# Another order, and a strict one, for the seven products of a Strassen-like matrix product

## The chip, the cores and the metric

The kernel runs on one core of one Trainium2 chip. The time is the device time of that core in microseconds (us). The engines are TensorE (PE, matmuls), VectorE (DVE), ScalarE (ACT), GpSimd (POOL) and SyncE (SP), whose queue issues most of the transfers. Each engine works through its own queue in a fixed order.

## The reference

A decoder trunk of two layers on 512 tokens with a model width of 1024. Each layer is a half-step feed-forward block, a mixing block with three kinds of attention, and a second half-step feed-forward block:

```python
def _swiglu(t, w_gate, w_up, w_down):
    return (jax.nn.silu(t @ w_gate) * (t @ w_up)) @ w_down

for l in range(DEPTH):
    f = _swiglu(_rmsnorm(h, ffn1_pre_g[l]), ffn1_w_gate[l], ffn1_w_up[l], ffn1_w_down[l])
    h = h + 0.5 * _rmsnorm(f, ffn1_post_g[l])
    ...   # mixing
    f = _swiglu(_rmsnorm(h, ffn2_pre_g[l]), ffn2_w_gate[l], ffn2_w_up[l], ffn2_w_down[l])
    h = h + 0.5 * _rmsnorm(f, ffn2_post_g[l])
```

`D_FF` is 2816, that is 22 blocks of 128 columns. All of it is in float32.

## The kernel before

**Precision.** A float32 factor is split into a high part (a cast on ScalarE, L182) and a low part (a subtraction on VectorE, L183). A product of two such factors is three matmuls, `mm3` (L203): high times high (L205), high times low weights (L206), low times high weights (L207).

**Seven products.** The first sixteen column blocks of a feed-forward block are computed as two chunks (`ci` 0 and 1) of 1024 columns. For each chunk, the gate and the up matrix product are done by a scheme with seven block products instead of eight, 0 to 6. This makes four groups of seven products in each feed-forward block, and there are four feed-forward blocks, named a0, c0, a1 and c1 in the tile names (so `pwc0g` is a bank of a gate group of block c0, `wh_gc` the high part of its weights). The block product with the down weights uses the same scheme (`product`, L851, tiles `pd`).

**Banks.** A product adds into a pair of PSUM banks. There are three pairs in a group: products 0, 3, 5 and 6 add into the first, 1 into the second, 2 and 4 into the third (`SUM`). After product 0 its two banks are copied to the second pair (L747). After each later product its pair is read out: copied by ScalarE after 2 and 3 (L775), added by VectorE after 4 and 5 (L777), and passed through the nonlinearity or multiplied after 1 and 6. A product that adds into a pair has to wait until the earlier read of that pair is done.

**Inputs.** Products 0, 1 and 6 take token blocks as they are (tiles `us`). Products 2, 3, 4 and 5 take sums of them (tiles `uh`, `ul`), which `sums` (L693) makes once per feed-forward block, step by step during the first group.

**Weights.** Each product has two units of weights (`BlockUnit`, L274), each 256 rows by 512 columns. A unit is fetched by a transfer on SP (L297), for products 2, 3, 5 and 6 combined with a kept block `t` by a subtraction on VectorE (L327), and split into `wh` and `wl`. Products 2 and 4 take over the raw block of 0 and 3. Raw blocks lie in two rings, `raw` with two buffers and `o` with four for this use; the kept blocks also have the tag `o`. The `wh` and `wl` tiles have four buffers each, that is two products. When a product begins, the next four units are loaded (`load_ahead`, L391), and when a raw buffer is released, the next unit in the order of the work is fetched if its ring has room (`fetch_ahead`, L411).

**Turned results.** The up groups hold their results with tokens on partitions; after products 1, 4, 5 and 6 they are transposed by transfers (`turn`, L790: copies L800, transposes L801 on SP, copies back L804 two products later). Products 1 and 5 use a tile with the tag `rs`, which has one buffer.

**The order of the work.** `PLAN` (L1643) lists the gate group of chunk 0, the up group of chunk 0, the gate group of chunk 1, the up group of chunk 1, then the down products with the remaining plain gate and up products between them. The program writes the instructions in this order, but the framework's scheduler may move an instruction ahead of others on its engine when it finds it ready sooner; a call of `keep_in_program_order` pins an instruction behind what was written before it on its engine.

Of the kernel before, what the change touches and what calls it, by code (L numbers as in the profile page):

```python
# [18 lines left out]
P = 128  # L19
# [4 lines left out]
def kernel(  # L24
# [85 lines left out]
    def pbank(tag, name):  # L110
        return ps.tile([P, S], F32, tag=tag, bufs=4, name=name)
# [88 lines left out]
        nc.vector.scalar_tensor_tensor(t, z, minus, t, ALU.max, ALU.add)  # L200
        nc.scalar.activation(t, t, AF.Exp, scale=-1.0, bias=minus)

    def mm3(pt, lh, ll, rh, rl, start, stop, free=False):  # L203

        nc.tensor.matmul(pt, lh, rh, start=start, stop=False, skip_group_check=free)  # L205
        nc.tensor.matmul(pt, lh, rl, start=False, stop=False, skip_group_check=free)  # L206
        nc.tensor.matmul(pt, ll, rh, start=False, stop=stop, skip_group_check=free)  # L207

# [386 lines left out]


    NG = 2
    ORDER = (0, 2, 1, 3, 4, 5, 6)
    SUM = (0, 1, 2, 0, 2, 0, 0)
    TO = ((0, 0), (0, 0), (1, 1), (0, 1), (0, 1), (1, 1), (1, 0))  # L600
    park = [nc.dram_tensor(f"park{i}", (NT, P, D), F32, kind="Internal").ap() for i in range(2 * L)]
# [1 line left out]
    def ffn(l, src, wg, wu, wd, dst, name, spare, parked, plan, aside=None):  # L603
# [136 lines left out]
        def token_product(ci, up, n, uns):  # L740

            nm = f"{name}{'gu'[up]}_{ci}_{n}"
            if n in (0, 1, 2):
                st["c", n] = [pbank("z" if n == 0 else "mm", f"pw{nm}_{e}") for e in range(2)]
            if n == 1:
                for e in range(2):
                    nc.scalar.copy(st["c", 1][e][:], st["c", 0][e][:])  # L747
            if n == 0:
                if not up:
                    st["s", ci] = {}  # L750
            pts = st["c", SUM[n]]
            h, l = in_product(n)
            opens, ends = n in (0, 2), n in (1, 4, 6)
            for un in uns:
                for k in range(un.nk):
                    kk = un.k0 + k
                    for e in range(2):
                        c = slice(e * P, (e + 1) * P)
                        mm3(pts[e][:], h[:, kk, c], l[:, kk, c], un.h[:, k], un.l[:, k], opens and kk == 0,
                            ends and kk == ND // 2 - 1, free=True)  # L760
                        yield 3 * S * PE_US
                    turn(kk)
            if n == 0:
                return
            q = TO[n]
            g = st["s", ci]
            if not up and q not in g:
                g[q] = stile([P, FC // 2, S // 2], "f", f"s{name}_{ci}_{q[0]}{q[1]}", F32)[:]
            g = g[q]
            r = hidden_rows(2 * ci + q[1])[:, :, HALVES[q[0]]] if up else g  # L770
            for e in range(2):
                p = pts[e][:].rearrange("p (f q) -> p f q", f=2)
                re, ge = r[:, 2 * e:2 * e + 2], g[:, 2 * e:2 * e + 2]
                if n in (2, 3):
                    nc.scalar.copy(re, p)  # L775
                elif n in (4, 5):
                    nc.vector.tensor_tensor(re, re, p, ALU.add)  # L777
                elif up:
                    nc.vector.tensor_tensor(ge, p, ge, ALU.mult)
                else:  # L780
                    nc.scalar.activation(re, p, AF.Silu)
            if n in (4, 5):
                if up:
                    nc.vector.tensor_tensor(g, r, g, ALU.mult)
                else:
                    nc.scalar.activation(r, r, AF.Silu)
            if up and n in (1, 4, 5, 6):
                turns.append([nm, g, (2 * ci + q[1], q[0]), n in (1, 5), 0, None])
# [21 lines left out]
        def token_products(ci, up):  # L810

            w, nm = (wu if up else wg)[l, :, ci * FC * P:(ci + 1) * FC * P], f"{'gu'[up]}{name}_{ci}"
            keep = Keep(lambda k0: stile([P, 2, S], "o", f"t{nm}_{k0}", F32)[:])
            places, had = itertools.cycle(("raw", "o", "o")), {}
            for n in ORDER:
                uns = [BlockUnit(n, w, ND // 2, k, 2, S, keep, f"{nm}_{n}_{k}", n in (2, 4) or next(places))
                       for k in range(0, ND // 2, 2)]
                if n in (2, 4):
                    for un, of in zip(uns, had[n - 2 + (n == 4)]):
                        un.inherits(of)  # L820
                had[n] = uns
                run = lambda n=n, uns=uns: token_product(ci, up, n, uns)
                early = ci == 0 and not up and n in ORDER[:4]
                yield uns, (lambda run=run: beside(run(), itertools.islice(st["some"], 1), 2)) if early else run

        def down_from(t, hf, pt):
# [24 lines left out]
        def product(at, uns):  # L851
# [10 lines left out]
            h, l = st.pop(("a", ci, n))  # L862
            opens, ends = first and n in (0, 2), last and n in (1, 4, 6)
            for un in uns:
                for k in range(un.nk):
                    kk = un.k0 + k
                    for e in range(2):
                        c = slice(e * P, (e + 1) * P)
                        mm3(pts[e][:], h[:, kk, c], l[:, kk, c], un.h[:, k], un.l[:, k], opens and kk == 0,
                            ends and kk == FC // 2 - 1, free=True)  # L870
                        yield 3 * S * PE_US
                    turn(kk)
            if not last:
                return
            if n == 0:
# [828 lines left out]
```

## Time and profile before

| | us |
|---|---|
| median of 3 runs | 2380.13 |
| the runs | 2378.37 to 2385.53 |
| the profiled execution | 2382.98 |
| its span, first to last instruction | 2380.9 |
| TensorE busy in the span | 2350.6 |
| VectorE busy | 1803.5 |
| ScalarE busy | 1513.8 |

The page gives the busy time of each engine; the list of waits says how long an engine stood idle before an instruction and what ended that; the timeline shows single instructions in order of time; windows give busy times of each engine in a stretch. Matmuls overlap in the trace: one row lasts 0.39 us, but the next begins before it ends, so the distance of the starts is what a matmul takes.

### The profile page before, as it was taken

The numbers are of one execution on the slowest core, as the hardware profiler recorded it, in microseconds if no ns is written. First come the engines' busy times: TensorE is split into PE (matmuls) and PEld (weight loads), VectorE is DVE, ScalarE is ACT, GpSimd is POOL, SyncE is SP. The second block draws the span as 40 slices with busy tenths as digits, with TensorE's granted clock in tenths as the row PEclk, the third lists the DMA queues.
The fourth block names the chain that finished last, engine by engine and source line by source line (L and its number), as shares of the span: only waits on it lengthen the run. The fifth ranks groups of instructions, "written<-read, shape, count | busy, mean of one in ns | idle before, by whom it ended". The sixth has DMA issues, their size and how long they took to land.

```text
span 2380.9 us, 31151 instructions
## 1 busy us (share of the span) xinstructions
PE 2350.6 (99%) x11719; PEld 1984.2 (83%) x11719; DVE 1803.5 (76%) x2358; ACT 1513.8 (64%) x2306; POOL 75.8 (3%) x134
## 2 busy tenths in 40 slices
PE   9999999999999999999999999999999999999998
PEld 7787889888888888778888878889888888888787
DVE  8886877667777689778788778766767767888785
ACT  6777465577766556775656665655777665567744
POOL 0000000000111000000000000000001100000000
PEclk9999999999999999999999999999999999999999
DMA  5666455223223556664647664542323235566643
GB/s 197 195 174 174 161 196 151 71 80 94 87 78 103 189 179 182 170 195 135 236 128 200 186 185 153 192 124 71 94 76 98 73 123 193 161 204 174 197 143 141
DMA packets 299754, 354.98 MB, mean 149 GB/s; under 512 B 78266, under 2 KB 192978, under 8 KB 299604
## 3 DMA queue, kind: packets, MB, share of 16 engines
q1 hardware_dynamic: 299508, 352.97, 48.0%
q8 instruction: 92, 1.51, 0.3%
q14 instruction: 58, 0.48, 0.1%
q0 software_dynamic: 96, 0.03, 0.0%
HBM read 319.39 MB, written 16.78 MB: 141 GB/s over the span
## 4 chain that ended last, share of the span: by engine, by line
PE 85%; DVE 5%; DMA 4%; ACT 4%; issue 2%; SPq 0%; DVEq 0%; ACTq 0%
PE pg L206 4%; PE pg L205 4%; PE pg L207 4%; PE pdc L206 3%; PE pdc L207 3%; PE pdc L205 3%; PE pda L206 2%; PE pda L207 2%; PE pda L205 2%; PE pb L207 2%; PE pb L206 2%; PE pb L205 2%; PE pq L206 1%; PE pq L205 1%; PE pk L207 1%
## 5 line engine op out<-in xcount | busy, mean ns | idle before, releaser
L205 PE MATMUL pg<-us_a,wh_wg 128*128 128x512 f32 x384 | 151.0, 393 | 0.0
L207 PE MATMUL pg<-us_a,wl_wg 128*128 128x512 f32 x384 | 149.8, 390 | 0.0
L206 PE MATMUL pg<-us_a,wh_wg 128*128 128x512 f32 x384 | 149.8, 390 | 0.0
L206 PE MATMUL pdc<-wl_dc,ahc 128*128 128x512 f32 x224 | 87.9, 392 | 3.6 <-DVE wl_dc L183 3.6
L206 PE MATMUL pda<-wl_da,aha 128*128 128x512 f32 x224 | 87.9, 392 | 3.6 <-DVE wl_da L183 3.6
L205 PE MATMUL pda<-wh_da,aha 128*128 128x512 f32 x224 | 86.8, 390 | 2.0 <-ACT wh_da L182 2.0
L205 PE MATMUL pdc<-wh_dc,ahc 128*128 128x512 f32 x224 | 86.8, 390 | 0.6 <-ACT wh_dc L182 0.6
L207 PE MATMUL pda<-wh_da,ala 128*128 128x512 f32 x224 | 87.3, 390 | 0.0
L207 PE MATMUL pdc<-wh_dc,alc 128*128 128x512 f32 x224 | 87.2, 389 | 0.0
L183 DVE TENSOR_TENSOR wl_da<-raw_da,wh_da 128x1024 fp32r<-128x1024 f32 x50 | 60.9, 1224 | 34.3 <-ACT wh_da L182 34.3
L207 PEld LDWEIGHTS pg<-us_a,wl_wg 128*128 128x128 f32 x384 | 72.1, 188 | 15.2
L206 PEld LDWEIGHTS pg<-us_a,wh_wg 128*128 128x128 f32 x384 | 72.2, 188 | 14.1
L205 PEld LDWEIGHTS pg<-us_a,wh_wg 128*128 128x128 f32 x384 | 72.1, 188 | 14.1
L183 DVE TENSOR_TENSOR wl_dc<-raw_dc,wh_dc 128x1024 fp32r<-128x1024 f32 x50 | 61.0, 1223 | 29.0 <-ACT wh_dc L182 28.9
L182 ACT CAST wh_da<-raw_da 128x1024 fp32r<-128x1024 f32 x50 | 52.2, 1050 | 45.6 <-PE pda L207 15.3
L182 ACT CAST wh_dc<-raw_dc 128x1024 fp32r<-128x1024 f32 x50 | 52.3, 1049 | 42.7 <-PE pdc L207 18.0
L186 DVE SCALAR_TENSOR_TENSOR wl_wg<-raw_wg,wh_wg 128x1024 fp32r<-128x1024 f32 x48 | 58.4, 1221 | 22.3 <-ACT wh_wg L185 22.3
L200 DVE SCALAR_TENSOR_TENSOR ga<-pg,bgate,ga 128x512 f32<-128x512 f32 x48 | 35.9, 747 | 50.5 <-ACT ga L199 50.5
L185 ACT ACTIVATE wh_wg<-raw_wg 128x1024 fp32r<-128x1024 f32 x48 | 50.5, 1057 | 24.6 <-PE pv L1096 11.7
L183 DVE TENSOR_TENSOR wl_uc<-raw_uc,wh_uc 128x1024 fp32r<-128x1024 f32 x44 | 53.7, 1220 | 16.2 <-ACT wh_uc L182 16.2
L183 DVE TENSOR_TENSOR wl_ua<-raw_ua,wh_ua 128x1024 fp32r<-128x1024 f32 x44 | 53.6, 1220 | 16.0 <-ACT wh_ua L182 16.0
L182 ACT CAST wh_uc<-raw_uc 128x1024 fp32r<-128x1024 f32 x44 | 46.1, 1050 | 30.4 <-PE pgc L206 7.6
(647 smaller groups left out, 8057.6 us busy)
## 6 DMA issues: line engine op xcount, KB each, us to landing
raw_da<-in_ffn_w_down_dram SPq DMA_DIRECT2D x66, 512.0 KB, 4.5
raw_dc<-in_ffn_w_down_dram SPq DMA_DIRECT2D x66, 512.0 KB, 3.9
raw_ga<-in_ffn_w_gate_dram SPq DMA_DIRECT2D x52, 512.0 KB, 4.2
raw_ua<-in_ffn_w_up_dram SPq DMA_DIRECT2D x52, 512.0 KB, 4.5
raw_gc<-in_ffn_w_gate_dram SPq DMA_DIRECT2D x52, 512.0 KB, 3.9
raw_uc<-in_ffn_w_up_dram SPq DMA_DIRECT2D x52, 512.0 KB, 3.6
raw_wg<-in_w_gate_dram SPq DMA_DIRECT2D x48, 512.0 KB, 3.6
raw_wo<-in_w_out_dram SPq DMA_DIRECT2D x24, 512.0 KB, 3.3
```

Of the source, the lines that this page charges most:

```text
L182: both = [nc.scalar.copy(h_ap, src)]
L183: make = lambda: nc.vector.tensor_tensor(l_ap, src, h_ap.bitcast(F32), ALU.subtract)
L185: both = [nc.scalar.activation(h_ap, src, AF.Copy, scale=scale)]
L186: make = lambda: nc.vector.scalar_tensor_tensor(l_ap, src, scale, h_ap.bitcast(F32), ALU.mult, ALU.subtract)
L200: nc.vector.scalar_tensor_tensor(t, z, minus, t, ALU.max, ALU.add)
L205: nc.tensor.matmul(pt, lh, rh, start=start, stop=False, skip_group_check=free)
L206: nc.tensor.matmul(pt, lh, rl, start=False, stop=False, skip_group_check=free)
L207: nc.tensor.matmul(pt, ll, rh, start=False, stop=stop, skip_group_check=free)
```

## The change

The first matmul of every product into each of its two banks is pinned behind all that was written before it on TensorE. In the gate groups and in the up group of chunk 0 the products are written as 0, 2, 3, 1, 5, 4, 6; the up group of chunk 1 keeps 0, 2, 1, 3, 4, 5, 6. Within a unit of weights the loop over the two banks is now outside the loop over the two row blocks, so six matmuls go into one bank and then six into the other, before it was three and three; this holds for the down products as well, which are pinned too. Which ring a unit's raw block uses is given by a table per product instead of a cycle. The copy of the first pair of banks to the second is written at the beginning of product 2 instead of product 1, and both other pairs are taken there.

```diff
-    def mm3(pt, lh, ll, rh, rl, start, stop, free=False):
+    def mm3(pt, lh, ll, rh, rl, start, stop, free=False, pin=False):
 
-        nc.tensor.matmul(pt, lh, rh, start=start, stop=False, skip_group_check=free)
+        one = nc.tensor.matmul(pt, lh, rh, start=start, stop=False, skip_group_check=free)
+        if pin:
+            tc.keep_in_program_order(one)
...
-    ORDER = (0, 2, 1, 3, 4, 5, 6)
+    ORDERS = ((0, 2, 3, 1, 5, 4, 6), (0, 2, 1, 3, 4, 5, 6))
+    PLACES = ("raw", "o"), ("raw", "o"), (None, None), ("o", "o"), (None, None), ("raw", "o"), ("raw", "o")
...
-            if n in (0, 1, 2):
-                st["c", n] = [pbank("z" if n == 0 else "mm", f"pw{nm}_{e}") for e in range(2)]
-            if n == 1:
+            for c in {0: (0,), 2: (2, 1)}.get(n, ()):
+                st["c", c] = [pbank("mm" if c else "z", f"pw{nm}_{c}{e}") for e in range(2)]
+            if n == 2:
                 for e in range(2):
                     nc.scalar.copy(st["c", 1][e][:], st["c", 0][e][:])
...
             for un in uns:
-                for k in range(un.nk):
-                    kk = un.k0 + k
-                    for e in range(2):
-                        c = slice(e * P, (e + 1) * P)
+                for e in range(2):
+                    c = slice(e * P, (e + 1) * P)
+                    for k in range(un.nk):
+                        kk = un.k0 + k
                         mm3(pts[e][:], h[:, kk, c], l[:, kk, c], un.h[:, k], un.l[:, k], opens and kk == 0,
-                            ends and kk == ND // 2 - 1, free=True)
+                            ends and kk == ND // 2 - 1, True, kk == 0)
                         yield 3 * S * PE_US
-                    turn(kk)
+                    turn(un.k0 + e)
...
-            places, had = itertools.cycle(("raw", "o", "o")), {}
-            for n in ORDER:
-                uns = [BlockUnit(n, w, ND // 2, k, 2, S, keep, f"{nm}_{n}_{k}", n in (2, 4) or next(places))
+            had, order = {}, ORDERS[ci and up]
+            for n in order:
+                uns = [BlockUnit(n, w, ND // 2, k, 2, S, keep, f"{nm}_{n}_{k}", PLACES[n][k // 2])
                        for k in range(0, ND // 2, 2)]
...
-                early = ci == 0 and not up and n in ORDER[:4]
+                early = ci == 0 and not up and n in order[:4]
```

The same exchange of the two loops and the same pin are in `product` (L851).

More of the change, by code (lines that the diff above doesn't have):

```diff
@@ L864, in product @@
             for un in uns:
[L865 to L868, printed above, removed]
+                for e in range(2):
+                    c = slice(e * P, (e + 1) * P)
+                    for k in range(un.nk):
+                        kk = un.k0 + k
                         mm3(pts[e][:], h[:, kk, c], l[:, kk, c], un.h[:, k], un.l[:, k], opens and kk == 0,
[L870 removed]
+                            ends and kk == FC // 2 - 1, True, kk == 0)
                         yield 3 * S * PE_US
[L872 removed]
+                    turn(un.k0 + e)
             if not last:
```

## The prediction

> **What bounds the kernel now.** The page first: how much of the span has TensorE (PE) idle, and what the chain that ended last consists of.
>
> ```profile
> span 2380.9 us, 31151 instructions
> PE 2350.6 (99%) x11719; PEld 1984.2 (83%) x11719; DVE 1803.5 (76%) x2358; ACT 1513.8 (64%) x2306; POOL 75.8 (3%) x134
> PE 85%; DVE 5%; DMA 4%; ACT 4%; issue 2%; SPq 0%; DVEq 0%; ACTq 0%
> ```
>
> TensorE is the bound, idle for only 2380.9 - 2350.6 = 30 us. The change leaves every matmul in place, so it can take back a part of those 30 us and some slow matmuls behind the waits, or add waits. Next the waits of TensorE inside the second feed-forward block's twenty-eight token products (four groups: gate and up of column chunk 0, gate and up of chunk 1; I call them G0, U0, G1, U1), after them the waits of the products with the down weights, and two from the first block, which only it has:
>
> ```profile
> PE pwc0u L206 <- DVE wl_uc L183: 0.8, 1, 0.8
> PE pwc0g L206 <- DVE wl_gc L183: 0.8, 1, 0.8
> PE pdc L206 <- DVE wl_dc L183: 0.8, 1, 0.8
> PE pwc0u L205 <- ACT wh_uc L182: 0.6, 1, 0.6
> PE pdc L205 <- ACT wh_dc L182: 0.4, 1, 0.4
> ...
> PE pdc L206 <- DVE wl_dc L183: 1.3, 1, 1.3
> ...
> PE pwa0g L207 <- DVE ula L183: 1.1, 1, 1.1
> PE pwa0u L205 <- ACT hra L775: 0.3, 1, 0.3
> ```
>
> Each wait for a weight comes once per group. The order of the matmuls at such a place says why; this is the timeline of TensorE at the border from G1 to U1 (start, duration, line, tiles, idle before), rows between left out:
>
> ```profile
> 987.08 0.39 PE L205 MATMUL pwc0g<-wh_gc,uhc 128*128 128x512 f32 x1
> ...
> 992.98 0.39 PE L207 MATMUL pwc0g<-wh_gc,ulc 128*128 128x512 f32 x1
> 993.92 0.50 PE L205 MATMUL pwc0u<-wh_uc,us_b 128*128 128x512 f32 x1 [0.56 <-ACT wh_uc L182]
> 995.18 0.50 PE L206 MATMUL pwc0u<-wl_uc,us_b 128*128 128x512 f32 x1 [0.76 <-DVE wl_uc L183]
> 995.78 0.50 PE L205 MATMUL pwc0g<-wh_gc,us_b 128*128 128x512 f32 x1
> ...
> 996.84 0.63 PE L205 MATMUL pwc0g<-wh_gc,us_b 128*128 128x512 f32 x1
> 997.27 0.63 PE L206 MATMUL pwc0g<-wl_gc,us_b 128*128 128x512 f32 x1
> ...
> 1002.96 0.39 PE L207 MATMUL pwc0u<-wh_uc,us_b 128*128 128x512 f32 x1
> ```
>
> From 987.08 to 992.98 there are 26 steps, so a matmul takes 5.90 / 26 = 0.227 us. Inputs `uh`, `ul` belong to products 2 to 5, `us` to 0, 1 and 6. After product 5 of G1 (last row 992.98) TensorE does not run product 6 of G1: it begins product 0 of U1, two matmuls, and waits for each factor of its weights. Only at 995.78 does product 6 run, with weights split long before. The matmuls that follow take 997.27 - 996.84 = 0.43 us, nearly twice the time. U0 to G1 has the same with four matmuls (953.94 to 955.77), and so has U1 to the down products:
>
> ```profile
> 953.60 0.39 PE L207 MATMUL pwc0u<-wh_uc,ulc 128*128 128x512 f32 x1
> 953.94 0.50 PE L205 MATMUL pwc0g<-wh_gc,us_b 128*128 128x512 f32 x1
> 955.20 0.50 PE L206 MATMUL pwc0g<-wl_gc,us_b 128*128 128x512 f32 x1 [0.76 <-DVE wl_gc L183]
> ...
> 956.00 0.39 PE L205 MATMUL pwc0u<-wh_uc,us_b 128*128 128x512 f32 x1
> ...
> 1034.92 0.39 PE L207 MATMUL pwc0u<-wh_uc,ulc 128*128 128x512 f32 x1
> 1035.66 0.50 PE L205 MATMUL pdc<-wh_dc,ahc 128*128 128x512 f32 x1 [0.36 <-ACT wh_dc L182]
> ...
> 1037.74 0.39 PE L205 MATMUL pwc0u<-wh_uc,us_b 128*128 128x512 f32 x1
> ```
>
> In the written order product 6 comes before the next group's 0; the scheduler of the framework moved it, because product 6 adds into the bank pair of product 5 and has to wait until VectorE (DVE) has read it. Here is that read (L777, two of 0.64 us) behind a weight split, on the timeline of DVE:
>
> ```profile
> 953.92 1.23 DVE L183 TENSOR_TENSOR wl_gc<-raw_gc,wh_gc 128x1024 fp32r<-128x1024 f32 x1 [0.67 <-ACT wh_gc L182]
> 955.07 1.28 DVE L777 TENSOR_TENSOR hrc<-hrc,pwc0u 128x512 f32<-128x512 f32 x2
> ```
>
> **What the moved matmuls cost.** Stretches from the first matmul of G0 to the last product 6 (columns: length, busy time of PE, of its weight loads, of DVE, ScalarE (ACT), POOL, clock, DMA):
>
> ```profile
> 38.93:201.98 163.05, 157.09 (x679) 127.56 (x677) 135.94 (x140) 120.98 (x138) 0.00 (x0) 0.99 0.60 167
> 882.76:1043.22 160.46, 157.18 (x679) 127.71 (x677) 133.42 (x128) 112.18 (x126) 0.00 (x0) 0.99 0.61 176
> 1223.56:1382.02 158.46, 155.48 (x678) 126.57 (x677) 133.67 (x128) 112.05 (x126) 0.00 (x0) 1.00 0.60 166
> 2063.07:2220.73 157.66, 155.09 (x678) 126.58 (x677) 133.31 (x128) 112.19 (x126) 0.00 (x0) 1.00 0.62 180
> ```
>
> In each lie 28 x 24 = 672 matmuls of the token products and four of the first down product (the other two or three counted are matmuls still running at the edges): 676 x 0.227 = 153.4 us. The excess is 9.7, 7.1, 5.1 and 4.3 us, together 26. Of it about 2 us are not at a border: the first block's waits for `ula` (1.1 and its restart, some 1.5) and `hra` (0.3, some 0.5). So **24 us hang on the matmuls moved across sixteen borders**. That is the most that the order alone can give back.
>
> **The change part by part.** *Order 0, 2, 3, 1, 5, 4, 6* in G0, U0, G1. Banks: product 5 still adds where 3 did, one product (1) between, as 4 lay between before; but 6 now has product 4, which adds into another pair, between it and 5. The 1.28 us read then has 24 x 0.227 = 5.4 us of cover. Nothing at P5 to P6 has to wait: 12 borders lose their reason.
>
> *Strict order.* Product 6 runs where it is written, and the next group's 0 starts 5.4 us less four matmuls later than its first matmul does now. At 953.94 that product's low part was made at 953.92 + 1.23 = 955.15; it would be wanted only after product 6, at about 959. So the same supply of weights is early by 4 us, and at 993.92 (low part wanted by 999, there at 995.18) too. I take the cost at these borders as 0; the cover is product 6 itself. If the splits came a whole product later, up to 1.4 us each would be paid.
>
> *U1 keeps its old order*, so there 6 follows 5 directly and now waits for the read. Bank 0 is finished six matmuls (1.36 us) before the product's end, not three, and bank 1 is wanted 1.36 us after the start of 6. A read of 0.64 us per bank fits if DVE is free; behind one split of 1.23 us it is late by some 0.5 us. Bounds: 0, and 1.9 us (the first of the two reads at 955.07 ended at 955.71, 1.9 us after the product's last matmul had gone through at 953.83). I take 0.5 x 4 = 2.0 us.
>
> *Six and six.* No matmul or weight load is added. A window with alternating banks and one with one bank throughout (a plain up product) last the same:
>
> ```profile
> 926.62:932.06 5.44, 5.44 (x25) 4.50 (x24) 5.08 (x6) 3.55 (x5) 0.00 (x0) 1.00 0.64 179
> 1082.00:1087.44 5.44, 5.44 (x26) 4.50 (x24) 4.53 (x4) 2.88 (x3) 0.00 (x0) 1.00 0.96 355
> ```
>
> So it costs 0 either way on TensorE; both parts of a unit's weights are needed in its first half as before.
>
> *G0 is the tight place.* There DVE also makes the summed inputs (`uh`, `ul`):
>
> ```profile
> 882.76:915.42 32.66, 32.66 (x146) 27.04 (x145) 32.53 (x32) 21.50 (x26) 0.00 (x0) 1.00 0.54 177
> ...
> 901.07 1.22 DVE L183 TENSOR_TENSOR wl_gc<-raw_gc,wh_gc 128x1024 fp32r<-128x1024 f32 x1
> ...
> 903.34 1.22 DVE L183 TENSOR_TENSOR ulc<-x11c,uhc 128x1024 fp32r<-128x1024 f32 x1
> ...
> 906.75 1.22 DVE L183 TENSOR_TENSOR ulc<-x00c,uhc 128x1024 fp32r<-128x1024 f32 x1
> ```
>
> DVE is busy for 32.53 of 32.66 us. Product 3 moves from fourth to third place and 5 from sixth to fifth (start 882.76 + 4 x 5.44 = 904.5). The input of 5 ends at 906.75 + 1.22 = 907.97; the two splits for product 4 (the last at 901.07) can now come behind it, 2 x 1.15 at the spacing of the rows 953.92 and 955.07, which gives 905.7: 1.2 us late. If the input for 4 (903.34) and its sum go behind too, it is in time. So 0 to 1.2 us for each G0, with a restart at half rate up to 2.8. I take 0.8 x 4 = 3.2 us.
>
> *Places, turns, copies.* Which ring a weight block lands in becomes a table; product 5 is loaded one product earlier, and with its release the fetch of the next group's first block on SP goes out one product (5.4 us) earlier and can only land sooner. The second fetch of the next group (the kept block) waits for product 3's buffer, now held until 4 has been split, and DVE's queue can stand behind that landing; it does so now (3.65 us below) without TensorE stopping for it alone. Each product's weights have a cover of about one product, 5.4 us. The copy of product 0's banks on ACT comes one product earlier; its cover, product 2, stays. In U0 the transposes on SP for products 1 and 5 share one buffer and now follow each other, so 5's wait for 1's copies: nothing needs them before the down products, but fetches stand behind them on SP. For these I take 2 us in all, between -2 (earlier fetch) and +8 (one 2 us stop per block).
>
> ```profile
> 984.88 1.23 DVE L327 TENSOR_TENSOR tuc<-tuc,raw_uc 128x1024 f32<-128x1024 f32 x1 [3.65 <-DMA tuc<-in_ffn_w_up_dram]
> ```
>
> *Down products* run in written order except at their first four matmuls; their inner wait for `wl_dc` (1.3) keeps its cause, cost 0.
>
> **Sum.** -24 + 2.0 + 3.2 + 2 = -17 us. The profiled execution took 2382.98 us (span 2380.9), 2.85 above the median 2380.13: 2366 for it, **2363 us** against the median.
>
> **Half rate.** This stretch holds the 993 border; the clock is the third number from the end:
>
> ```profile
> 993.20:1002.96 9.76, 8.35 (x28) 6.13 (x27) 4.92 (x6) 4.21 (x5) 0.00 (x0) 0.83 0.64 197
> ```
>
> Here idle waits of 0.56 + 0.76 us sufficed for a stretch at 0.43 us a matmul: product 6 took 1002.96 - 995.78 = 7.2 us instead of 5.4, most of it the slow rate, some 1.6 us. So a new stop is priced at its length + 1.6. The Trainium skill, "TensorE: Matmul & The Clock Gate", Part 1, says the clock falls to half after at least one idle window of about 3.4 us; by that rule a 2 us stop would cost 2 alone. The trace does not bear it out (1.3 us of idle was enough), so the price with the restart stands.
>
> **The rivals.** *First groups give half back*: each G0 stops at product 3 and at 5, 1.2 us each, and one of them restarts at half rate: 4.0 x 4 = 16 in place of 3.2, so 2363 + 13 = 2376. For it: 32.53 of 32.66. Against: product 1's two splits fall away before 3.
>
> *Nothing changes*: the splits slip with the order, and the strict order waits at the same borders for the same splits: 2380. Against: at 955.15 the weight was there 4 us before it would be wanted.
>
> *Slower*: in strict order any late split stops TensorE, and products 2 and 3, with two subtractions each (L327), stand next to each other in all twelve groups. If every such pair makes one stop of 1.1 us with a half-rate restart of 1.6, that is 12 x 2.7 = 32 us against the 24: 2380 + 8 + 2 = 2390. It decides from 2.0 us per group on. For it: the 3.65 us in which DVE stood behind a fetch. Against: the list of waits of the second block has none inside U0 and G1, only at their borders. By the skill's rule above the restart would not come: 12 x 1.1 = 13, and the time about 2371.
>
> **How the numbers follow.** What can be told from no change is some 0.3%, 7 us: below 2373 is faster, above 2387 slower. Forecast (2354 to 2370) 0.54; half given back (2368 to 2378) 0.16, of it half still faster; nothing changes 0.08; slower 0.22. Faster 0.54 + 0.08 = 0.62, same 0.08 + 0.08 = 0.16, slower 0.22. The range goes from 2354 (all 24 and the 2 us of earlier fetches back) to 2390, into the slower case; the likeliest case's own range is 2354 to 2370.
>
> **What would show it.** Right: product 6 directly behind 4 in G0, U0, G1; no matmul of the next group ahead of it; no waits for `wh` or `wl` at borders; the four stretches between 154 and 157 us; no rows of 0.63 us in them. Wrong: waits for `wl_g` or `ul` at the third and fifth place of G0; waits for `wh`/`wl` inside U0 or G1 behind transposes or the kept block; a stop before product 6 of U1 over 1 us; time lost in mixing or down products, which I hold at zero.

## The result and the profile after

The changed kernel takes 2405.91 us (2403.56 to 2407.26) where the kernel before, on the same chip, takes 2379.77 us: a ratio of 1.0106 (95% interval 1.0089 to 1.0123). It is slower by about 25 us. The prediction was 2363 us and faster, with a range up to 2390.

The page of the profiled execution (2404.9 us of span, 24.0 more than before):

```profile
span 2404.9 us, 31137 instructions
PE 2355.9 (98%) x11719; PEld 1988.1 (83%) x11719; DVE 1803.7 (75%) x2358; ACT 1512.5 (63%) x2306; POOL 75.5 (3%) x134
```

TensorE has the same 11719 matmuls, but is now idle for 49 us instead of 30, and busy for 5 us longer, since more of them run slowly behind a stop. The same windows as in the prediction, from the first matmul of G0 to the last of U1 (columns as there):

```profile
38.67:203.66 164.99, 156.35 (x675) 126.68 (x674) 136.09 (x140) 120.33 (x138) 0.00 (x0) 0.99 0.59 165
887.15:1049.78 162.63, 155.94 (x674) 127.58 (x673) 134.26 (x128) 112.00 (x126) 0.00 (x0) 0.98 0.60 174
1230.88:1394.67 163.79, 156.20 (x674) 127.39 (x673) 134.12 (x128) 111.75 (x126) 0.00 (x0) 0.98 0.58 161
2076.92:2240.58 163.66, 156.07 (x675) 126.70 (x673) 134.38 (x128) 112.10 (x126) 0.00 (x0) 0.99 0.61 173
```

They are together 655.1 us, before 639.6. They no longer hold the four matmuls of the first down product (16 x 0.227 = 3.6 us less work), so the loss in them is 15.4 + 3.6 = 19 us; the other 5 us are between the stretches, 4 of them in longer waits of the down products. Beyond 672 x 0.227 = 152.5 us of work, the stretches now hold 12.5, 10.1, 11.3 and 11.2 us, 45 in all, where before there were 26. The list of waits of TensorE says at which places (total, count, longest):

```profile
PE pwa0u L205 <- ACT aha L182: 4.3, 1, 4.3
PE pwc0u L205 <- ACT ahc L182: 4.0, 1, 4.0
PE pwc1u L205 <- ACT ahc L182: 3.8, 1, 3.8
PE pwa1u L205 <- ACT aha L182: 3.8, 1, 3.8
PE pda L208 <- DVE wl_da L183: 3.5, 2, 2.6
PE pdc L208 <- DVE wl_dc L183: 3.3, 2, 2.3
PE pwa0g L209 <- DVE ula L183: 2.2, 2, 1.3
PE pwc0g L209 <- DVE ulc L183: 1.9, 2, 1.5
PE pwa1g L209 <- DVE ula L183: 1.9, 2, 1.5
PE pwc1g L209 <- DVE ulc L183: 1.9, 2, 1.5
PE pwc1g L205 <- DVE sc L780: 1.5, 1, 1.5
PE pwa1g L205 <- DVE sa L780: 1.4, 1, 1.4
```

The waits for `wh` and `wl` at the borders of the groups are gone, as forecast. In their place stand one wait of about 4 us in each U1, the waits of G0 for its summed inputs (`ul`), and waits of G1 before product 6. This is the place in U1 of block c0, product 5 into product 6, on TensorE:

```profile
1037.45 0.39 PE L209 MATMUL pwc0u<-wh_uc,ulc 128*128 128x512 f32 x1
1041.80 0.77 PE L205 MATMUL pwc0u<-wh_uc,us_b 128*128 128x512 f32 x1 [3.97 <-ACT ahc L182]
1042.37 0.63 PE L208 MATMUL pwc0u<-wl_uc,us_b 128*128 128x512 f32 x1
...
1046.21 0.63 PE L208 MATMUL pwc0u<-wl_uc,us_b 128*128 128x512 f32 x1
1047.05 0.39 PE L205 MATMUL pwc0u<-wh_uc,us_b 128*128 128x512 f32 x1
```

Idle from 1037.68 to 1041.80, then matmuls 0.43 us apart until 1047.05: product 6 takes 8.0 us instead of 5.4. With its slow matmuls this stop costs 6.7 us; the other three (a0, a1, c1) cost 6.2, 6.4 and 5.7, together **24.9 us**, of which 8.4 are slow matmuls. I had put 2.0 on the four. VectorE at the same place:

```profile
1038.14 1.22 DVE L183 TENSOR_TENSOR alc<-hrc,ahc 128x1024 fp32r<-128x1024 f32 x1
1039.84 1.23 DVE L183 TENSOR_TENSOR wl_dc<-raw_dc,wh_dc 128x1024 fp32r<-128x1024 f32 x1 [0.48 <-ACT wh_dc L182]
1040.98 1.28 DVE L780 TENSOR_TENSOR hrc<-hrc,pwc0u 128x512 f32<-128x512 f32 x2
```

The last row is the read of product 5's banks (L777 before). Its banks were ready at 1037.9, but in VectorE's order it stands behind two splits for the down products, and the second waits for ScalarE. Half of its 1.28 us is over at 1041.6, and product 6 begins 0.2 us later. The row of TensorE names the cast `ahc` as what it waited for; the experiment below that takes the read away shows that it is the read. ScalarE in turn was held by the turned rows and, behind them, worked without a gap:

```profile
1034.69 1.37 ACT L807 COPY hrc<-trc0u 128x1024 uint16<-128x1024 uint16 x1 [1.56 <-DMA trc0u<-thc0u]
...
1037.82 1.03 ACT L803 COPY thc0u<-sc 128x1024 uint16<-128x1024 uint16 x1
1038.76 1.04 ACT L182 CAST wh_dc<-raw_dc 128x1024 fp32r<-128x1024 f32 x1
```

The kernel before has the same order there. Its ScalarE and VectorE:

```profile
1034.56 1.05 ACT L182 CAST wh_dc<-raw_dc 128x1024 fp32r<-128x1024 f32 x1
...
1035.64 1.23 DVE L183 TENSOR_TENSOR wl_dc<-raw_dc,wh_dc 128x1024 fp32r<-128x1024 f32 x1 [0.47 <-ACT wh_dc L182]
1036.79 1.28 DVE L777 TENSOR_TENSOR hrc<-hrc,pwc0u 128x512 f32<-128x512 f32 x2
```

Counted from the first matmul of G0, that cast begins at 1034.56 - 882.76 = 151.8 us before and at 1038.76 - 887.15 = 151.6 us after. TensorE has finished product 5 at 1035.15 - 882.76 = 152.4 before and at 1037.68 - 887.15 = 150.5 after. So in this block TensorE came 1.9 us earlier to a supply that had not moved, and it had lost the four down matmuls with which it had filled the time. The other blocks are not all like it. This is when TensorE is done with product 5 of U1 and when VectorE begins to read its banks, in us from the first matmul of G0, worked out in the same way:

| block | done, before | read begins, before | done, after | read begins, after |
|---|---|---|---|---|
| a0 | 153.8 | 156.6 | 153.4 | 157.0 |
| c0 | 152.4 | 154.0 | 150.5 | 153.8 |
| a1 | 150.3 | 152.0 | 151.9 | 155.1 |
| c1 | 149.8 | 151.3 | 152.5 | 155.7 |

In a0 and c0 TensorE comes earlier to a read that has hardly moved; in a1 and c1 TensorE comes later, and the read later still, by 3.0 and 4.4 us. What the four share is that the read begins 3.1 to 3.6 us after product 5, where it was 1.5 to 2.9 before, and that nothing fills the time. Why the read came later in a1 and c1 was not traced.

### The profile page after: what moved, and what is told of

Same layout as the page of the kernel before. It is cut to its first block, busy times and chain, and to the rows that moved or that the text cites. A ratio compares the mean times of both kernels' runs of the same rounds, so it can differ in the third digit from the quotient of the medians.

```text
span 2404.9 us, 31137 instructions
## 1 busy us (share of the span) xinstructions
PE 2355.9 (98%) x11719; PEld 1988.1 (83%) x11719; DVE 1803.7 (75%) x2358; ACT 1512.5 (63%) x2306; POOL 75.5 (3%) x134
## 4 chain that ended last, share of the span: by engine, by line
PE 78%; DMA 7%; DVE 6%; ACT 5%; issue 3%; SPq 0%; DVEq 0%; POOL 0%; ACTq 0%
PE pg L208 4%; PE pg L205 4%; PE pg L209 4%; PE pdc L208 3%; PE pdc L209 3%; PE pdc L205 3%; PE pda L208 2%; PE pda L209 2%; PE pda L205 2%; PE pb L209 1%; PE pb L208 1%; PE pb L205 1%; PE pq L208 1%; PE pq L205 1%; PE pk L208 1%
## 5 line engine op out<-in xcount | busy, mean ns | idle before, releaser
L209 PE MATMUL pg<-us_a,wl_wg 128*128 128x512 f32 x384 | 149.8, 390 | 0.0
L208 PE MATMUL pg<-us_a,wh_wg 128*128 128x512 f32 x384 | 149.8, 390 | 0.0
L182 ACT CAST wh_dc<-raw_dc 128x1024 fp32r<-128x1024 f32 x50 | 52.1, 1050 | 44.3 <-PE pdc L209 15.7
```

The source lines that it names most:

```text
L182: both = [nc.scalar.copy(h_ap, src)]
```

## The experiments

Ratios are those to the kernel before on the same chip; 0.1% is 2.4 us. The expectations are in us on the chip of the result, where the kernel before takes 2380; on the chips of the experiments it takes 2384 to 2387, so a measured time has to be compared by its ratio. Costs of stops include the slow matmuls behind them. Theory A: the loss is the strict order at products 5 and 6 together with the late read. Theory B: the new order, loops and places cost by themselves.

**The pin taken from U1 alone.**

```diff
-  ends and kk == ND // 2 - 1, True, kk == 0)
+  ends and kk == ND // 2 - 1, True, kk == 0 and not (ci and up))
```

> The changed kernel, with the pin left off in U1 (up group of chunk 1) only. Theory A (strict order in U1, where product 6 directly follows 5, makes TensorE wait for the read of 5's banks, which VectorE does only behind other splits: 6.2, 6.7, 6.4 and 5.7 us there in the four blocks, against some 2 us each before): four matmuls of the first down product run in that gap again, about 17 us less, 2389. Theory B (the new order and places in the other groups make weights late, and the strict order has little to do with it): within 5 us of 2406.

Measured 2414.41 us, ratio 1.012 (1.010 to 1.014): a miss. The down product was still pinned behind product 6, so nothing could fill the gap, and the scheduler put five matmuls of product 1 ahead of product 2, which stopped TensorE for another 3.3 to 6.1 us in each block. It does not tell the theories apart.

**The new order in U1 too.**

```diff
-  had, order = {}, ORDERS[ci and up]
+  had, order = {}, ORDERS[0]
```

> The changed kernel, U1 too in the order 0, 2, 3, 1, 5, 4, 6, strict everywhere. Theory A (it is the neighbourhood of 5 and 6 that costs, not strictness as such): the stop before product 6 of U1 goes, some 23 us less, 2383. Theory C (strict order by itself costs some 6 us in the last group, since the first down product's splits and turns crowd ScalarE and VectorE there): about 2406, with the stop elsewhere in U1.

2390.51 us, ratio 1.0025 (1.0014 to 1.0036), so some 19 us of the loss are gone. No wait is left in U1, and the stretches last 158.8, 155.5, 157.4 and 160.1 us, together 631.8, which is 4 us less than before (639.6, less 3.6 for the sixteen down matmuls). But the stretches between them became longer, by about 10 us, with waits of the down products of 1.9 to 6.2 us (slow matmuls included) where before there were 1.0 to 1.6. VectorE at the longest, the fourth down product of block c1:

```profile
2239.49 1.22 DVE L841 TENSOR_TENSOR asc<-hrc,hrc 128x1024 f32<-128x1024 f32 x1
2240.87 1.23 DVE L329 TENSOR_TENSOR btc<-btc,raw_dc 128x1024 f32<-128x1024 f32 x1 [0.15 <-DMA raw_dc<-in_ffn_w_down_dram]
2243.72 1.22 DVE L329 TENSOR_TENSOR btc<-btc,raw_dc 128x1024 f32<-128x1024 f32 x1 [1.63 <-DMA raw_dc<-in_ffn_w_down_dram]
```

Ahead of the split for this product VectorE makes a sum of turned rows and two subtractions, the second after 1.63 us of waiting for a transfer. What U1 gained was partly waited for in the next stage.

**No pin anywhere in the changed kernel, and the pin alone in the kernel before.**

```diff
-  if pin:
+  if False:
```

> The changed kernel with no pin at all: new order, table of places, six and six remain. Theory A: U1 is as before the change (2 us per block), G0, U0, G1 have no reason to move matmuls; G0 and G1 keep their stops (11 and 10 us in sum): 2386 to 2390. Theory B (new order and places are to blame): about 2406.

```diff
-  ends and kk == ND // 2 - 1, free=True)
+  ends and kk == ND // 2 - 1, free=True, pin=kk == 0)     # and the same in the down products
```

> The kernel before with the pin alone: old order 0, 2, 1, 3, 4, 5, 6 everywhere, old places, three and three. Theory A: each of the sixteen borders has product 6 behind 5 and pays the read: some 6 us in the four U1, 2 to 4 us in the other twelve, less the 24 us of now: 2395 to 2430. Theory B (new order to blame, pin harmless): within 5 us of 2380.

2420.52 us, 1.0147 (1.013 to 1.0164), and 2409.81 us, 1.0105 (1.0085 to 1.0125). The pin alone, in the old order and with the old loops, costs all that the change costs. Without it the new order is slower still: the scheduler then moves other matmuls, and product 3 of G1 waits up to 5.9 us for the copy of product 0's banks (L750). So the parts do not add up, and in the old order the matmuls moved ahead were no loss: forbidding it costs 25 us. Its two longest waits when pinned, in a0's U0 and c0's U1:

```profile
PE pwa0u L205 <- ACT wh_ga L182: 3.7, 1, 3.7
PE pwc0u L205 <- ACT ahc L182: 3.5, 1, 3.5
```

**Six and six alone,** in the kernel before.

```diff
-  for k in range(un.nk):                        # in the token and in the down products
-      kk = un.k0 + k
-      for e in range(2):
+  for e in range(2):
+      for k in range(un.nk):
+          kk = un.k0 + k
```

> The kernel before with the six-and-six loops alone: old order, nothing pinned. Theory A (all of the loss comes from what the strict order does at products 5 and 6, the loops are free): 2380, between 2375 and 2387, the four stretches of token products within 2 us of those before (163.1, 160.5, 158.5, 157.7). Theory B (the loops cost by themselves, because a unit's low factor or a bank is wanted earlier): over 2390, with new stops inside groups and not at their borders.

2384.03 us, 0.9993 (0.9981 to 1.0005). The loops cost nothing, as forecast.

**The first down product free to fill again.**

```diff
-  ends and kk == FC // 2 - 1, True, kk == 0)
+  ends and kk == FC // 2 - 1, True, kk == 0 and at > 0)
```

> The changed kernel with the pin taken from the first down product alone: product 6 of U1 stays behind product 5, but four matmuls of the first down product may run between them, as they did before. Theory A (the stop of 5.6 to 6.7 us before product 6 of U1 is the late read of product 5's banks, and what the strict order took away is only what filled that time): the four stops fall to what the same place cost before (2.9, 1.7, 1.7, 1.5 us), 17 us less: 2389, between 2383 and 2394. Theory B (the stop comes from loops, places or late weights): the four matmuls move but a stop of over 4 us stays: 2400 or more.

2396.43 us, 1.0043 (1.0027 to 1.0059): 15 us come back, about what Theory A expected, but not at this place: it still costs 5.2, 6.4, 5.1 and 5.1 us, against the 1.5 to 2.9 expected. The profiled execution, the slowest of the six, is only 6 us shorter than that of the changed kernel, so where the rest lies it does not show. The four matmuls now wait for their own weights:

```profile
1037.19 0.39 PE L209 MATMUL pwc0u<-wh_uc,ulc 128*128 128x512 f32 x1
1039.81 0.50 PE L205 MATMUL pdc<-wh_dc,ahc 128*128 128x512 f32 x1 [2.23 <-ACT wh_dc L182]
1041.07 0.79 PE L208 MATMUL pdc<-wl_dc,ahc 128*128 128x512 f32 x1 [0.76 <-DVE wl_dc L183]
...
1042.09 0.63 PE L205 MATMUL pdc<-wh_dc,ahc 128*128 128x512 f32 x1
1042.51 0.63 PE L205 MATMUL pwc0u<-wh_uc,us_b 128*128 128x512 f32 x1
```

Before, the first of these waits was 0.36 us (row 1035.66 of the prediction). At the place itself Theory A is right in direction and far short in size.

**The read of product 5 taken away from U1.**

```diff
+  seen = st["c", 2] if ci and up and n == 5 else pts
-  p = pts[e][:].rearrange(...)
+  p = seen[e][:].rearrange(...)
```

> The changed kernel, where in U1 alone the addition after product 5 reads product 4's pair of banks, which is long done, in place of product 5's, so product 6 has no read to wait for (this leaves out what product 5 adds, so the output is another one); order, pins, loops and places stay. Theory A: the four stops (24.8 us) before product 6 of U1 go, at most 1 us each is left, and the down product behind them may lose some 1 to 2 us each by asking for its weights earlier: 2384, between 2379 and 2392. Theory B (product 6 waits for its weights or its input, not for the bank): stops of over 3 us stay there, 2400 or more.

2395.74 us, 1.0044 (1.0028 to 1.006). The ratio lies at the upper end of what Theory A allowed (2390 of 2379 to 2392). The stops in U1 are gone, which shows that the wait was for the bank:

```profile
1036.27 0.39 PE L209 MATMUL pwc0u<-wh_uc,ulc 128*128 128x512 f32 x1
1036.49 0.39 PE L205 MATMUL pwc0u<-wh_uc,us_b 128*128 128x512 f32 x1
```

But the likeliest value was 2384, 6 us less, and of the 24.9 us taken away only some 15 came back. The down products took back the rest, waiting for ScalarE to copy their banks:

```profile
PE pdc L205 <- ACT pdc L882: 5.4, 2, 3.5
PE pda L205 <- ACT pda L882: 5.3, 2, 2.8
```

**The old order in G0 besides** (first down product free, first product of U0 free).

```diff
-  had, order = {}, ORDERS[ci and up]
+  had, order = {}, ORDERS[ci == up]
```

> As the kernel with the first down product unpinned, and besides G0 keeps the old order 0, 2, 1, 3, 4, 5, 6 with the first product of U0 unpinned, so that its matmuls may fill behind product 5 of G0; U0 and G1 keep the new order, strict. Theory A (the new order in G0 costs the stops for the summed inputs at the third and the fifth place, 2.5 us per block, and the borders into G1 and U1 are worth some 8 net): 10 less than the kernel with the first down product unpinned alone, 2379, between 2373 and 2384, with no stop on a summed input in the blocks a1, c0, c1. Rival: the old order in G0 brings stops at the border to U0 instead (1 to 2 us each plus the half rate), and the time stays within 3 us of that kernel's.

2392.85 us, 1.0036 (1.0023 to 1.0048), 0.07% below the kernel without this edit, which is inside the intervals. In c0, a1 and c1 the stops for `ul` are gone and the stretches are 3.5, 1.0 and 1.1 us shorter; in a0 the stretch is 2.4 us longer. The 2.5 us per G0 are a real stop, but not a loss of that size.

**Product 4 directly behind 3.** Theory C: the new order keeps product 3's raw blocks for two more products, so the next group's kept blocks are fetched later, and this makes the supply late. Theory D: the supply of U1 is what it is, and TensorE waits there for whatever it gained earlier.

```diff
+  ORDERS = (..., (0, 2, 3, 4, 5, 1, 6))      # for U0 and G1; first down product free
```

> As the changed kernel with the first down product unpinned, but U0 and G1 take their products as 0, 2, 3, 4, 5, 1, 6: the bank pairs still alternate at every step, and product 4 stands directly behind product 3 again, whose raw blocks it inherits, so these buffers come free one or two products earlier. Theory C (the new order keeps product 3's two raw blocks for two more products, so the next group's kept blocks are fetched some 7 us later against TensorE, VectorE's queue stands behind their landing, and the supply arrives late at product 6 of G1 and again at the first down product after U1): in c0, a1 and c1 the stops before product 6 of G1 (1.7 each) go, the waits for the high factor of the first down product fall from 2.2 us to under 1, together 4 to 5 us per block: 2380, between 2374 and 2388. Rival D (the supply is late because TensorE no longer stops at the earlier borders, whatever the order): the stops at U1 stay 5 us per block, 2393 or more.

> The same, with G0 in the old order 0, 2, 1, 3, 4, 5, 6 and the first product of U0 unpinned. Theory C: the stops for summed inputs in G0 (2.5 us per block in c0, a1, c1) go as well, one wait of 0.5 us at U0's first low factor comes in: 2375, between 2368 and 2382, so faster than the kernel before. Rival D: 2389 or more.

2398.16 us, 1.0068 (1.0046 to 1.009), and 2390.14 us, 1.0024 (1.0013 to 1.0034). The stops before product 6 of G1 went, but new ones came (0.4 to 2.3 for the copy L750, 1.2 to 2.9 mostly for reads on ScalarE, L778), and the first down product still waits 1.3 to 2.6 us for `wh`. As a whole G1 holds 16.9 and 16.0 us of stops, against 11.2 and 12.1 in the two kernels without this order. Theory C falls: the order moved the stops and saved nothing that can be told from zero. Theory D fits the first run; the second is 3 us faster than it allowed.

**Twelve matmuls more at the beginning of U1.**

```diff
+  for _ in range(12 if ci and up and n == 0 else 0):
+      tc.keep_in_program_order(nc.tensor.matmul(pts[0][:], h[:, 0, 0:P], uns[0].h[:, 0], start=True, stop=False, ...))
```

> The changed kernel with twelve more matmuls (12 x 0.227 = 2.7 us) at the beginning of product 0 of U1, into a bank that product 0 then overwrites, so the result is the same: 10.9 us more work for TensorE in the four blocks. Theory D (in U1 the supply of factors sets the time, and what TensorE gains at the earlier borders it waits for at product 6 of U1): the added work is taken up by shorter stops there and fewer slow matmuls, at least 8 of the 10.9 us: 2402 to 2409. If TensorE is the bound in U1 and the stop is a fixed wait behind product 5: 2417.

2415.44 us, 1.0113 (1.0089 to 1.0137), against 1.0106 without them: 10.9 us of added work on TensorE cost about 2 us, with an interval of some 7 us to both sides: nothing that can be told from zero. The four waits before product 6 shrank:

```profile
PE pwa0u L205 <- ACT aha L182: 2.9, 1, 2.9
PE pwa1u L205 <- ACT aha L182: 2.7, 1, 2.7
PE pwc0u L205 <- ACT ahc L182: 2.5, 1, 2.5
...
PE pwc1u L205 <- ACT ahc L182: 2.1, 1, 2.1
```

From 15.9 us of idle to 10.2, and the stops as a whole from 24.9 to 15.7; the four U1 together last 1.7 us longer. (The stretches last 6.6 us longer, but 5 of these are in G1, ahead of the added matmuls.) Theory D holds in the main: at this place the supply sets the time more than TensorE does. It is not quite fixed, since from the start of U1 the read came 1.0 to 1.6 us later; and about a third of the added work was taken up by fewer slow matmuls: 4.9 us of them are left, nearly all in a1 and c1.

**What holds the supply.** Theory E: ScalarE, which stands in its order for the transposing transfers in front of the splits. First the changed kernel without the transposes, then both kernels with the copies back moved to GpSimd.

```diff
-  part = tmp(...); nc.scalar.copy(part, words[:, h::2])
-  nc.sync.dma_start_transpose(plane.rearrange(...), part)
+  nc.scalar.copy(plane, words[:, h::2])
```

> The changed kernel, in which the turning of the up products' rows leaves out the transposing DMA: ScalarE copies the words straight into the buffer the DMA would have filled, and back as before (so the output is another one); all copies, orders and pins stay. Theory E (ScalarE works in order, and its copies out of the turned buffers stand 0.8 to 1.8 us for the transposing DMA in front of the splits of U1 and of the first down product; that lateness is what TensorE meets in U1 and behind it): the stops before product 6 of U1 fall from 6.2 to under 3 us each, 2390, between 2382 and 2396. If the transposes do not matter: 2400 to 2408.

2389.84 us, 1.0011 (0.9999 to 1.0024): 23 us hang on the transposes, as much as nearly the whole loss. The kernel before was not run without them, so it is not shown that they cost it less. And the expected place was missed: the idle waits in U1 fell only to 2.8 to 3.1 us, and with the slow matmuls the stops there still cost 5.0, 4.8, 4.7 and 5.9 us, not under 3. The rest came from G1, whose stops fell from 9.5 to 4.5 us, and from the down products, whose waits fell from 9.5 to 1.7.

```diff
-  nc.scalar.copy(r[:, :, i * S + kk:...], planes[kk]...)
+  nc.gpsimd.tensor_copy(r[:, :, i * S + kk:...], planes[kk]...)
```

> The changed kernel, with the two copies out of the turned buffers moved from ScalarE to GpSimd, which is idle for 97% of the span; nothing is left out. Theory E: ScalarE no longer stands for the transposing DMA and saves 2.7 us of copies per turned product, the splits of U1 and of the down products come 2 to 4 us earlier: 2390, between 2380 and 2398. Against it: these copies may take GpSimd several times the 1.36 us that ScalarE takes, and if the rows are then late for the down products, or VectorE is slowed beside it, 2405 or more.

> The kernel before with the same move of the two copies to GpSimd. Theory E: its waits for the splits at the borders into G1, U1 and the down products (some 20 us with the slow matmuls behind them) shrink by a third to a half: 2373, between 2366 and 2379, faster than both. If the rows come late, or ScalarE was not the cause: 2380 to 2395.

2423.33 us, 1.0148 (1.0125 to 1.017), and 2421.0 us, 1.0139 (1.0112 to 1.0167): both missed what Theory E promised, and the stops in U1 grew, to about 7 us each in the changed kernel. The trace says why: ScalarE still stands, now with the cast `ahc` of a row that GpSimd has to copy first, and the splits of U1 and of the down products stand behind that cast. In c0 of the changed kernel:

```profile
1044.91 1.34 POOL L807 COPY hrc<-trc0u 128x1024 uint16<-128x1024 uint16 x1 [3.65 <-DMA trc0u<-thc0u]
1046.28 1.05 ACT L182 CAST ahc<-hrc 128x1024 fp32r<-128x1024 f32 x1 [5.81 <-POOL hrc L807]
```

In the four U1 of both kernels this wait lasts 4.9 to 5.8 us, where in the changed kernel itself ScalarE stood 1.56 us for the transfer (row 1034.69). So the move did not free ScalarE but held it longer, and the supply came later: that fits Theory E, whose promise rested on a freed ScalarE.

**The copies back one product later,** in both kernels, nothing left out.

```diff
-  if kk in (0, 1) and age == 2:
+  if kk in (0, 1) and age == 3:
```

> The kernel before, with the copies out of the turned buffers one product later in program order, so ScalarE stands less for the transposing DMA; nothing is left out. Theory E: its waits for that DMA (0.8 to 1.8 us each, about four per block) go, the splits of G1, U1 and the first down product come 1 to 3 us earlier, and the stops there shrink by 1 to 3 us per block: 2373, between 2367 and 2380. Against it: the rows of chunk 1 are late for the down products, 2385 or more.

> The changed kernel with the same later copies. Theory E: 8 to 15 us less, as leaving out the transposes gave 22 less: 2394, between 2388 and 2400. If only the load on the DMA queues mattered and not the order on ScalarE: 2402 to 2408.

The kernel before: 2386.44 us, 1.0001 (0.9988 to 1.0014), no change, so the expectation for it missed. The changed kernel: 2398.42 us, 1.005 (1.0035 to 1.0065), 13 us less. In the changed kernel the stops in G1 fell from 9.5 to 2.2 us (before product 6 from 0.6 to 1.7 us to at most 0.7), those in U1 stayed at 5.3 to 6.5. Theory E is right for the changed kernel, but not by way of U1. This pair also shows what the run without transposes leaves open: that ScalarE stands for the transfers costs the changed kernel something and the kernel before nothing that can be seen.

**The split of the first down weights later.** Theory F: product 6 of U1 waits because the read stands in VectorE's order behind the splits for the down product.

```diff
   for un in self.jobs[i][0]:
-      un.load()
+      if getattr(un, "late", False) and i > self.at + 1: un.fetch()
+      else: un.load()                           # late: the units of the first down product
```

> The changed kernel, where the split of the first down product's weights is put one product later in program order, so on VectorE the read of product 5's first bank in U1 comes ahead of both splits, and the second bank's behind one instead of ahead of none. Theory F (product 6 of U1 waits because the read stands in VectorE's order behind a split whose high factor ScalarE makes late): the stops before product 6 fall from 6.2 us to 1 to 3 us each; the first down product may then wait 1 to 2 us for its own factors: 2393, between 2386 and 2400. Theory D alone (whatever is taken out of that place is waited for right behind it): 2400 to 2408, with the time at the first down products.

2396.43 us, 1.0043 (1.0026 to 1.0059), 15 us less. VectorE in c0; TensorE had finished product 5 at 1034.8:

```profile
1036.23 0.68 DVE L783 TENSOR_TENSOR hrc<-hrc,pwc0u 128x512 f32<-128x512 f32 x1
1036.83 1.22 DVE L183 TENSOR_TENSOR wl_dc<-raw_dc,wh_dc 128x1024 fp32r<-128x1024 f32 x1
```

```profile
1037.06 0.47 PE L205 MATMUL pwc0u<-wh_uc,us_b 128*128 128x512 f32 x1 [2.10 <-DVE hrc L783]
1037.37 0.40 PE L208 MATMUL pwc0u<-wl_uc,us_b 128*128 128x512 f32 x1
1037.60 0.39 PE L209 MATMUL pwc0u<-wh_uc,us_b 128*128 128x512 f32 x1
```

The read comes ahead of the down split, the wait falls from 4.0 to 2.1, and in c0, a1 and c1 the slow matmuls behind it nearly vanish: the four stops cost 4.7, 2.4, 2.7 and 2.3 us, half of what the changed kernel loses there; a0 alone stays above the 3 us expected. Theory F holds for this half.

**All three repairs at once** (later split, later copies, old order of G0 in c0, a1, c1).

> The changed kernel with three repairs at once: the later split of the first down weights, the turned copies one product later, and in the blocks c0, a1 and c1 the old order of G0, with the first product of U0 free to fill behind its product 5. If the parts add up (0.63%, 0.56% and some 0.1% of the 1.06%): 0.998 of the kernel before, 2375 to 2384, within 0.3% of it or just faster. If the supply of U1 binds whichever part is repaired (Theory D): they don't add up, and 1.002 to 1.005 stays.

2385.48 us, 1.0001 (0.9992 to 1.001). The repairs bring the whole loss back, 0.2% less than their parts add up to, and no more: the stretches of c0, a1 and c1 last 156.3, 157.2 and 155.5 us, nearly as short as I had forecast, but the down products behind them wait again:

```profile
PE pdc L208 <- DVE wl_dc L183: 5.4, 2, 2.9
```

No version was faster than the kernel before by more than its interval.

## Why the prediction was wrong

**"That is the most that the order alone can give back", 24 us.** The borders did what was forecast: in G0, U0 and G1 product 6 follows 4, nothing is moved ahead, and no border has a wait for `wh` or `wl`. But the 24 us were not lost *by* the moved matmuls, which filled time in which TensorE would have waited: the kernel before with nothing but the pin was 1.05% slower. And what the borders gave back was waited for behind them. Twelve more matmuls in U1 cost next to nothing, and with the new order in U1 too, so with no stop left there, the stretches were only 4 us shorter than before and the rest 10 us longer. The argument held the lateness at the borders for a result of the early start. In U1 it comes from ScalarE and VectorE: counted from the first matmul of G0, the read was at most 0.2 us earlier in any block, and 3.0 and 4.4 us later in two.

**"U1 keeps its old order", 0.5 x 4 = 2.0.** This is the step that failed: the wait for the read was taken as 0.5 us, and it was about 4 in each block; with the slow matmuls the term measured 24.9 us. My upper bound, 1.9 us for each, was read off the border from U0 to G1, where one split stood ahead of the read. At the place itself, the rows 1035.64 and 1036.79 of the kernel before show the read behind a down split that itself waits for ScalarE, its first half over at 1037.43, 2.3 us after product 5. The term did not use these rows; the four down matmuls hid the wait (the row of product 6 at 1037.74 has none). I also did not add the slow matmuls to this term, though I had priced a new stop at "its length + 1.6". The moved work was the cover of this place, and the cover was taken away. With what was measured in place of each term, the sum comes out: -24 + 24.9 here, 9 in G0, 9.5 in G1 and 4 in the down products are 23 us, and the profiled execution became 24 us longer.

**"G0 is the tight place", 0.8 x 4 = 3.2.** Right place and right mechanism: waits for `ul` at the third and the fifth product. The size was 2.5 us per block in c0, a1 and c1 and 3.2 in a0, where 1.6 had been there before: 9 us more in all, near my upper bound of 2.8 each. Taking it out gave hardly anything back: probably it, too, only shifts when TensorE meets U1, but that was not shown apart.

**"Places, turns, copies", 2 us.** G1 has 9.5 us of stops now, among them 0.6 to 1.7 before each product 6. Most of them went when the turned copies came later. That is above my bound of 8 us as well as my value.

**"Six and six" 0 and "Down products" 0.** The first was right (0.9993). The second was wrong by 4 us: the waits for `wl_d` grew from 5.3 to 9.5 us with the slow matmuls, and the repairs in U1 made them larger still (13.8 us with the new order there, 13.3 with the three repairs, 10.1 with the later split alone).

**The rivals.** "Slower" gave 2390 by the pair of products 2 and 3 stopping in twelve groups. No wait for these weights appears at that pair: G0 stops there for its summed input, a0 in G1 once for the copy L750, and U0 has no stop at all. It was slower for another reason, which I had listed only among the signs of being wrong: "a stop before product 6 of U1 over 1 us". The half rate behind short waits, on which that rival's price stood against the Trainium skill's rule ("TensorE: Matmul & The Clock Gate", Part 1, one idle window of some 3.4 us), showed again: in the first down product unpinned, waits of 2.23 and 0.76 us, both under that window, were followed by matmuls 0.42 us apart (1042.09 to 1042.51).

What stays open: why the first down products take back what is won in U1 in so many forms (a late sum, a late fetch, a late copy), why the read in U1 came later in a1 and c1, and how much of the 23 us without the transposes the kernel before would gain too.

## What to carry to other kernels

Work that a scheduler has moved ahead of its place may be the filling of a wait, not its cause; before crediting the undoing of such a move, look at the same rows on the other engines and ask what TensorE would do there with nothing else to run. Before counting a stop as a gain, add a few harmless matmuls ahead of it: if the time does not grow, the supply is the bound there, and what is saved at that stop is likely to be waited for elsewhere. Where a step is hidden in the profile of before, take its bound from that very place, not from one that looks alike.

## What the runs showed of the hardware

The half rate does not go by the length of a wait alone. In the experiment with the later split, a wait of 2.10 us was followed by steps of 0.31 and then 0.23 us, which is full rate. In the kernel before, two waits of 0.56 and 0.76 us, with two matmuls between them, were followed by steps of 0.43 us, and so was the wait of 3.97 us in the changed kernel, by ten of them. With the twelve matmuls added, waits of 2.9, 2.5, 2.7 and 2.1 us at the same place of the blocks a0, c0, a1 and c1 were followed by 0.1, 0.1, 3.0 and 1.7 us lost to slow matmuls. It was not tried what decides.

A copy of 128 x 1024 words of 16 bits took 1.36 us on ScalarE; on GpSimd it took 1.3 to 2.4 us, 1.7 to 1.8 on average. In that run the splits of the down weights on VectorE took 1.27 us on average instead of 1.22, and one that ran partly beside a GpSimd copy of 1.99 us took 1.78.
